# The second query-key product of two heads on 64 rows each, with the heads of a pair taking turns by unit

## Chip, cores and metric

The kernel runs on one core of one Trainium2 chip. The metric is the device time of one execution in microseconds (us). Several runs were made, and the median counts. The profile is of one execution and has its own time.

The engines are called TensorE (PE in the profile, PEld for its weight loads), VectorE (DVE), ScalarE (ACT), GpSimd (POOL) and SyncE (SP). SyncE here only issues DMA transfers.

## The reference: what is computed

It is one encoder block on a sequence of 1024 tokens of width 1024, all in float32. The core of it, shortened:

```
h = einsum('bsd,de->bse', x, w_in)              # one combined projection
q_a, k_a, v_a, z_a, q_b, k_b, v_b, z_b = split(h)
y_a = neighborhood_attention(q_a, k_a, v_a, rel_pos_bias)   # 8 heads of 64
y_b = windowed_gqa_with_sink(rotary(q_b), rotary(k_b), v_b, sink)  # 8 query, 2 key heads of 64
mixed = concatenate([y_a * silu(z_a), y_b * silu(z_b)])
x = layer_norm(alpha * x + mixed @ w_out, gain, bias)
```

Group A sees the tokens as a grid of 16 rows by 64 columns. Each query attends to a window of 8 rows by 16 columns, clamped inside the grid, with a learned bias for each relative position. Group B attends to keys at most 128 positions away, with rotary positions on q and k, and with one learned sink logit for each head that takes part in the softmax sum and brings no value.

## The kernel before

**Precision.** A float32 operand is split into a high and a low part in f16, h + l, and a product a * b is computed as three matmuls: ah * bh, ah * bl and al * bh. In the query-key product this is done in another way, which the change touches. A head has 64 dimensions, TensorE has 128 rows. For every head `split_q` (line 293) writes the high part of q into one half of a tile's 128 partitions and the low part into the other half. Head j = 0 of a pair has its high part in partitions 0 to 63, head j = 1 in 64 to 127. `split_k` (line 307) writes the high part of k into the tile `kh` and the low part into the tile `kl`, each in one half, and then copies each into the other half on GpSimd (`dup_`, line 317, the copy itself in line 319). So one matmul of the stacked q against `kh` (line 910) gives qh * kh + ql * kh, and a second one against `kl` (line 911) gives qh * kl + ql * kl. Both read all 128 rows.

**Units.** Attention is done in 128 units, listed by `unit_list` (line 837). First come 64 of group B: head pair p = 0 to 3, in it head j = 0 and 1, in it the eight blocks t of 128 queries. A unit of group B has 384 keys, and 256 for the first and the last block. Then come 64 of group A: pair p, head j, four column blocks b of 16 columns, and two halves of eight grid rows. A unit there has 11 or 12 rows of 24 or 32 columns, so 264, 288, 352 or 384 keys. In the code before, all units of a head stand together.

**Steps.** A hand-written loop (line 1271) walks over steps i, one unit a step, and fixes the order of instructions on every engine. What a step issues around the change:

- `stage_qk` (line 888): takes a PSUM bank of the kind "s", of which there are four (`bank`, line 80), runs the two query-key matmuls, and on VectorE one instruction (L920) that adds the bias or mask and takes the row minimum of the negated scores into `sn` and `nm`.
- `stage_exp` (line 926): the exponential on ScalarE (L936), which writes back into the same bank.
- `stage_tr` (line 939), one step later: ScalarE and VectorE split the probabilities into f16 parts (L946 and L947), and a DMA transposes them into the tile `tr` (L950). When L947 has ended, the bank is free for the unit four steps on.
- `stage_pv` (line 957): every fourth step, nine steps after a quad's first unit, 33 or 36 matmuls of the transposed probabilities with the values for a quad of four units (L975).
- `stage_on` (line 977) divides by the softmax sums, `stage_ot` (line 987) transposes two heads' outputs on TensorE (L995) and multiplies the gate in (L998, L1004).
- `pump_to` (line 1013): TensorE's fill, which is the matmuls of the projections still to come (L405, 512 columns each), and at the end the first of the output projection (L1122). `FILL_AT` says at which step each of them begins.

Other work waits in lists for ACT, DVE, POOL and SP, from which each step takes a few instructions (`pop`, line 173). `need` (line 183) issues at once what a step depends on: the splits of q and k of the head in lines 1307 to 1310, and the scaling of the bias tile in line 900.

**Loads.** `stage_load` (line 869) runs seven steps ahead. For group A it loads a bias tile at the first half of column blocks 0, 1 and 3 (block 2 shares the tile of block 1), and GpSimd scales it (L882). There are five bias buffers (`BR`). `gather_v` (line 830) loads the values of the next pair's column blocks, at the steps that `VA_STEP` names.

After the steps, `final` (line 1139) finishes the output projection and the layer norm.

The lines that a sentence can't say:

```
        nc.tensor.matmul(ps[:, :m], q, sl[0], start=True, stop=False)      # line 910
        nc.tensor.matmul(ps[:, :m], q, sl[1], start=False, stop=True)      # line 911
```

Of the kernel before, what the change touches and what calls it, by code (L numbers as in the profile page):

```python
# [17 lines left out]
HD = 64  # L18
# [5 lines left out]
NEG = -1e30  # L24
PSCALE = 2.0 ** 14
QSCALE = 2.0 ** -15
LTT, LPP, BP, BH, BR, ND, NA, NX, F1 = 1, 6, 2, 9, 5, 1, 1, 6, 0.2
NSPLIT, NP = 6, 2
ORDER = ["zb0", "z0", "zb1", "kb", "qb0", "z1", "qb1", "zb2", "qb2", "k0", "qb3", "zb3", "q0", "k1", "q1",
         "k2", "q2", "k3", "q3", "z2", "z3"]  # L30
# [12 lines left out]
Z3_END = 119  # L43
WIN_AT = [186, 202, 218, 234]
VA_AT = [46, 49, 52, 55]
VA_STEP = [(0, 1, 1), (0, 1, 3), (1, 0, 1), (1, 0, 3)]
WO_TAG = ("wor", "wor", "raw", "raw") + ("wr",) * 5 + ("wor", "wor", "raw", "raw", "raw", "wr", "wr")
M_AT = [105, 112, 118, 120]
WO_PRE = (9, 10, 12, 13, 14, 15)
# [18 lines left out]
def hybrid_block(ctx, tc, xT, x, wt, wv, wo, bias, sink, gain, lbias, cos, sin, bmask, out):  # L68
# [238 lines left out]
    def split_k(p, half, src, dep=None):  # L307
        sl = slice(512 * half, 512 * half + 512)
        ops = []
        prio = 0 if dep is None else 1  # L310
        eng = "pool" if dep and clock["step"] is not None else "dve"
        for j in range(2):
            a, o = slice(64 * j, 64 * j + 64), slice(64 - 64 * j, 128 - 64 * j)
            hi, lo = split_hl(lambda j=j, a=a: own("kh", p, j)[a, sl], lambda j=j, a=a: own("kl", p, j)[a, sl],
                              src[a], dep is None, eng)

            def dup_(w, j=j, a=a, o=o):
                t = own(w, p, j)
                nc.gpsimd.tensor_copy(t[o, sl], t[a, sl])  # L319

            o1 = enq("act", hi, dep, prio=prio, after=28 if dep else 0)
            o2 = enq(eng, lo, o1, prio=prio, after=32 if dep else 0)
            ops.append(o2)
            dup = [enq("pool", lambda d=dup_: d("kh"), o1, after=32 if dep else 0),
                   enq("pool", lambda d=dup_: d("kl"), o2, after=36 if dep else 0)]
            stk_ops.setdefault((p, j, half), []).extend(dup)
        return ops

# [508 lines left out]
    def unit_list():  # L837
        us = []
        for p in range(4):
            for j in range(2):  # L840
                for i in range(8):
                    us.append(("b", p, j, i, i % 2 == 1))
        for p in range(4):
            for j in range(2):
                for b in range(4):
                    for half in range(2):
                        us.append(("a", p, j, (b, half), half == 1))
        return us
# [9 lines left out]
    on = {}  # L858

    def geom(u):  # L860
        g, p, j, t, _ = u
        if g == "a":
            b, half = t
            w = WINW[b]
            return NKEY[b], [4 * w] * 3
        lo, hi = max(t - 1, 0), min(t + 2, 8)
        return 128 * (hi - lo), [128] * (hi - lo)

    def stage_load(u, i):
        g, p, j, t, _ = u  # L870
        n, _c = geom(u)
        if g == "a":
            b, half = t
            if half == 0 and b != 2:
                bulk["last"] = clock["step"] + 1
                bt = ap.tile([128, 23 * WINW[1]], F32, tag="bs", name="bias", bufs=BR)
                o, m = BOFF[b], 23 * WINW[b]
                nc.sync.dma_start(bt[:, :m], bias[2 * p + j, :, o:o + m])
                bv = bt[:, :m]
                ld = Op("sp", None, [], 1)  # L880
                ld.step = i
                op = enq("pool", lambda: nc.gpsimd.tensor_scalar(bv, bv, rsg, -1.0, op0=ALU.mult, op1=ALU.mult),  # L882
                         ld, prio=0)
                st["bias"] = bt, op
            o = 11 * WINW[b] * half
            st[u, "b"] = st["bias"][0][:, o:o + NROW[half] * WINW[b]], st["bias"][1]

    def stage_qk(u):
        g, p, j, t, _ = u
        n, _c = geom(u)  # L890
        ps = bank("s")
        m, end = n, 384
        if g == "a":
            b, half = t
            m, end = NROW[half] * WINW[b], 384 if half else 384 - WINW[1]
            q = stks["q", p, j][:, 512 * half + 128 * b:512 * half + 128 * b + 128]
            sl = [stks[w, p, j].rearrange("p (r c) -> p r c", c=GW)[
                :, 4 * half:4 * half + NROW[half], WIN0[b]:WIN0[b] + WINW[b]] for w in ("kh", "kl")]
            bias_t, op = st.pop((u, "b"))
            need(op)  # L900
            init = 3e38
        else:
            q = stks["q", f"b{p}", j][:, 128 * t:128 * t + 128]
            lo = max(t - 1, 0) * 128
            kv = p // 2
            sl = [stks[w, "b", kv][:, lo:lo + n] for w in ("kh", "kl")]
# [3 lines left out]
        nc.tensor.matmul(ps[:, :m], q, sl[0], start=True, stop=False)  # L910
        nc.tensor.matmul(ps[:, :m], q, sl[1], start=False, stop=True)  # L911
        s0 = sns[units.index(u) % 2]
        sn = s0[:, end - m:]
        if g == "b" and t < 2:
            nc.vector.tensor_copy(s0[:, 384:385], nsk[:, h:h + 1])
        elif units.index(u) == 64:
            nc.vector.memset(s0[:, 384 - WINW[1]:384], -NEG)
        nm = ap.tile([128, 1], F32, tag="nm", name="nm", bufs=6)
        c = min(p, 1) if g == "b" else 2
        nc.vector.tensor_tensor_reduce(sn[:, :m], ps[:, :m], bias_t, sg[:, c:c + 1], init,  # L920
                                       op0=ALU.add, op1=ALU.min, accum_out=nm)
        st[u, "sn"] = sn
        st[u, "ps"] = ps
        st[u, "nm"] = nm

    def stage_exp(u):
        n, _c = geom(u)
        m = n + 1 if u[0] == "b" else n
        sn, nm = st.pop((u, "sn")), st.pop((u, "nm"))
        pt = st.pop((u, "ps"))  # L930
        k = units.index(u) % 4
        if k == 0:
            st["sm"] = ap.tile([128, 4], F32, tag="sm", name="sm", bufs=4)
        sm = st["sm"]
        st[units.index(u) // 4, "sm"] = sm
        nc.scalar.activation(pt[:, :m], sn[:, :m], AF.Exp, bias=nm, scale=-1.0, accum_out=sm[:, k:k + 1])  # L936
        st[u, "p"] = pt

    def stage_tr(u):
        g, p, j, t, _ = u  # L940
        n, ch = geom(u)
        pt = st.pop((u, "p"))
        c, m = ch[0], len(ch)
# [7 lines left out]
        st[u, "tr"] = tr  # L951

    def quad(q):
        g, p, j, t, _ = units[4 * q]
        return g, p, j, t // 4 if g == "b" else t[0] // 2

    def stage_pv(q):
        ps = st[q, "o"] = bank("t")
        for m in range(4):
            u = units[4 * q + m]  # L960
            g, p, j, t, _ = u
            n, ch = geom(u)
            tr = st.pop((u, "tr"))
            c = ch[0]
# [1 line left out]
            for i in range(len(ch)):  # L966
# [4 lines left out]
                    v = [vb[:, max(t - 1, 0) + i, p // 2, e, :] for e in range(2)]  # L971
                ph, pl = tr[:c, 2 * i, :], tr[:c, 2 * i + 1, :]
                mms += [(ph, v[0]), (ph, v[1]), (pl, v[0])]
            for i, (a, b_) in enumerate(mms):
                nc.tensor.matmul(ps[:, HD * m:HD * m + HD], a, b_, start=(i == 0), stop=(i == len(mms) - 1))  # L975

    def stage_on(q):
        g, p, j, h = quad(q)
        ps = st.pop((q, "o"))
        ri = ap.tile([128, 4], F32, tag="ri", name="ri", bufs=4)  # L980
        nc.vector.reciprocal(ri, st.pop((q, "sm")))
        if j == 0:
            on[g, p, h] = ap.tile([128, 4, 2, HD], F32, tag="on", name="on", bufs=2)
        nc.vector.tensor_mul(on[g, p, h][:, :, j, :], ps[:, :4 * HD].rearrange("p (m e) -> p m e", e=HD),
                             ri.unsqueeze(2).to_broadcast([128, 4, HD]))

    def stage_ot(q):
        g, p, j, h = quad(q)
        if j == 0:
            return  # L990
        need(*stk_ops.get(f"zb{p}" if g == "b" else f"z{p}", ()))
        ps = bank("t")
        o = on.pop((g, p, h))
        for i in range(4):
            nc.tensor.transpose(ps[:, 128 * i:128 * i + 128], o[:, i].rearrange("p h e -> p (h e)"), identf)  # L995
# [275 lines left out]
    for i in range(-LD, NU + LO):  # L1271
# [31 lines left out]
        if bulk["last"] != i or (queues["sp"] and i - queues["sp"][0].born > 2):  # L1303
            pop("sp", 1 if i < 118 else 3)
        if i < NU:
            u = units[i]
            if u[3] in (0, 4):
                need(*stk_ops[f"b{u[1]}", u[2], u[3] // 4])
            if u[3] == (0, 0):
                need(*stk_ops[u[1], u[2], 0], *stk_ops[u[1], u[2], 1])  # L1310
            stage_qk(u)
        q, m = divmod(i - LP - 3, 4)
        if i >= Q30 + 2:
            q, m = (NU // 4 - 2, i - Q30 - 2) if i < Q30 + 4 else divmod(i - LP - 3, 4)
        elif i >= Q30:
            q, m = -1, 0
        if m == 0 and 0 <= q - 1 < NU // 4:
            stage_ot(q - 1)
        if m == 0 and 0 <= q < NU // 4:
            stage_pv(q)  # L1320
        if i > Z3_END:
# [9 lines left out]
            wo_scale(i - WO_MAX - 4)  # L1331
        pump_to(i + F1)
        if 0 <= q < NU // 4:
            g, p, j, h = quad(q)
            if g == "a" and p < 3 and (j, h, m) in VA_STEP:
                gather_v(p + 1, VA_STEP.index((j, h, m)))
        if m == 1 and 0 <= q < NU // 4:
            stage_on(q)
        turned = pop("dve", ND if i < M_AT[1] else 2)
# [85 lines left out]
```

## Time and profile before

| what | value |
|---|---|
| median of 3 runs | 447.07 us (446.6 to 447.26) |
| the profiled execution | 447.43 us |
| its span in the profile | 445.6 us |
| mean granted TensorE clock | 0.998 |
| units' query-key matmuls, first and last start | 123.5 and 356.7 us |

The span is what the trace covers of the profiled execution; the rest of its time lies around it. Instruction rows of the profile name the line of the kernel, the engine, the operation, output <- inputs by the program's tile names, the shape, and a count. In a group of instructions the numbers behind the bar are the busy time in us, the mean duration of one in ns, then the idle time of the engine ahead of them and what ended it. In the timeline the first number is the start in us from the span's start, the second the duration of the row, in which matmuls that follow each other directly are merged. In a table of windows each engine has its busy time, and in brackets its number of instructions; the last columns are the granted clock, the DMA share and GB/s. A matmul's end is modelled, so the distance from one start to the next says more than its duration.

### The profile page before, as it was taken

The numbers are of one execution on the slowest core, as the hardware profiler recorded it, in microseconds if no ns is written. First come the engines' busy times: TensorE is split into PE (matmuls) and PEld (weight loads), VectorE is DVE, ScalarE is ACT, GpSimd is POOL, SyncE is SP. The second block draws the span as 40 slices with busy tenths as digits, with TensorE's granted clock in tenths as the row PEclk, the third lists the DMA queues.
The fourth block names the chain that finished last, engine by engine and source line by source line (L and its number), as shares of the span: only waits on it lengthen the run. The fifth ranks groups of instructions, "written<-read, shape, count | busy, mean of one in ns | idle before, by whom it ended". The sixth has DMA issues, their size and how long they took to land.

```text
span 445.6 us, 9522 instructions
## 1 busy us (share of the span) xinstructions
PE 438.6 (98%) x3271; PEld 254.3 (57%) x3271; DVE 345.7 (78%) x862; ACT 309.0 (69%) x718; POOL 227.0 (51%) x240
## 2 busy tenths in 40 slices
PE   9999999999999999999999999999999999999994
PEld 8996754444445555565655655655555654444442
DVE  5969967829989787786898888897767747279954
ACT  6769459877488998798979978797886876002211
POOL 0002753565837758868507628667762446005740
PEclk9999999999999999999999999999999999999999
DMA  8972068976847887678989999999999888101721
GB/s 306 348 286 94 1 242 270 298 268 238 285 138 165 149 179 163 141 146 133 165 164 173 194 182 184 201 188 239 189 189 229 156 190 323 49 0 71 253 79 71
DMA packets 133984, 81.76 MB, mean 183 GB/s; under 512 B 101296, under 2 KB 113328, under 8 KB 133680
## 3 DMA queue, kind: packets, MB, share of 16 engines
q1 hardware_dynamic: 133504, 80.67, 74.1%
q8 instruction: 25, 0.41, 0.4%
q10 hardware_dynamic: 432, 0.49, 0.3%
q14 instruction: 23, 0.19, 0.2%
HBM read 50.73 MB, written 9.96 MB: 136 GB/s over the span
## 4 chain that ended last, share of the span: by engine, by line
PE 88%; DMA 6%; ACT 3%; DVE 1%; issue 0%; SPq 0%; ACTq 0%; DVEq 0%
PE ps_pj L405 47%; PE ps_s L1122 9%; PE ps_t L975 7%; PE ps_pj L1122 5%; PE ps_t L1122 5%; PE ps_s L910 4%; PE ps_s L911 4%; PE ps_s L662 3%; PE ps_t L995 2%; PE ps_t L662 1%; DMA wos<-in_wo 1%; PE ps_pj L662 1%; DMA wr<-in_wt 1%; DMA x<-in_xT 1%; ACT wf L511 1%; DMA wvraw<-in_wv 1%
## 5 line engine op out<-in xcount | busy, mean ns | idle before, releaser
L405 PE MATMUL ps_pj<-xf,wh 128*128 128x512 f16 x672 | 202.6, 379 | 0.1
L405 PE MATMUL ps_pj<-xf,wl 128*128 128x512 f16 x336 | 127.3, 379 | 0.0
L405 PEld LDWEIGHTS <-wh 128*128 128x128 f16 x672 | 63.9, 98 | 60.3 <-issue 0.5
L936 ACT ACTIVATE ps_s<-sn,nm 128x385 f32<-128x385 f32 (+3 forms) x128 | 70.0, 547 | 28.9 <-DVE nm L920 27.8
L947 DVE SCALAR_TENSOR_TENSOR split<-ps_s,split 128x384 f16<-128x384 f32 (+2 forms) x128 | 65.6, 512 | 16.9 <-ACT split L946 16.0
L1122 PEld LDWEIGHTS <-m 128*128 128x128 f16 x408 | 38.8, 98 | 42.7 <-issue 0.2
L946 ACT ACTIVATE split<-ps_s 128x384 f16<-128x384 f32 (+2 forms) x128 | 57.6, 450 | 2.4
L405 PEld LDWEIGHTS <-wl 128*128 128x128 f16 x336 | 32.9, 98 | 36.7
L920 DVE CUSTOM_DVE_ANT_0 sn<-ps_s,bias,sg 128x264 f32<-128x264 f32 (+1 forms) x64 | 35.2, 549 | 15.8 <-PE ps_s L911 5.3
L212 POOL TENSOR_SCALAR wr<-wr,wsc 128x512 f32<-128x512 f32 x26 | 22.1, 851 | 41.1 <-ACT wh L207 35.5
L920 DVE CUSTOM_DVE_ANT_0 sn<-ps_s,bm,nsk 128x384 f32<-128x384 f32 (+1 forms) x64 | 40.7, 636 | 1.8 <-PE ps_s L911 1.3
L1122 PE MATMUL ps_s<-wo,m 128*128 128x512 f16 (+1 forms) x192 | 42.0, 372 | 0.0
L910 PE MATMUL ps_s<-ks,qs 128*128 128x384 f16 (+4 forms) x128 | 39.2, 306 | 0.0
L882 POOL TENSOR_SCALAR bias<-bias,rsg 128x552 f32<-128x552 f32 (+1 forms) x24 | 18.7, 779 | 40.3 <-DMA bias<-in_bias 32.0
L911 PE MATMUL ps_s<-ks,qs 128*128 128x384 f16 (+4 forms) x128 | 39.2, 306 | 0.0
L975 PEld LDWEIGHTS <-tr 128*128 128x128 f16 (+1 forms) x1104 | 36.6, 98 | 2.2
L1179 ACT ACTIVATE sd<-mv,eps 128x1 f32<-128x1 f32 x8 | 2.4, 295 | 44.3 <-DVE mv L1177 42.0
L213 POOL TENSOR_TENSOR wl<-wr,wh 128x512 f16<-128x512 f32 x26 | 31.6, 1215 | 2.2
L1221 POOL TENSOR_TENSOR xr<-xr,gb 128x512 f32<-128x512 f32 x7 | 11.2, 1608 | 39.7 <-ACT xr L1218 39.7
L319 POOL COPY ks<-ks 64x512 f16<-64x512 f16 x40 | 26.0, 662 | 4.7 <-DVE ks L289 1.8
L558 POOL TENSOR_SCALAR xraw<-xraw,xsc 128x512 f32<-128x512 f32 x3 | 4.9, 1645 | 41.0 <-ACT xf L553 41.0
L1122 PE MATMUL ps_pj<-wo,m 128*128 128x512 f16 (+1 forms) x120 | 25.2, 347 | 0.0
(208 smaller groups left out, 840.3 us busy)
## 6 DMA issues: line engine op xcount, KB each, us to landing
ws<-in_wt SPq DMA_DIRECT2D x15, 512.0 KB, 5.7
wr<-in_wt SPq DMA_DIRECT2D x26, 256.0 KB, 3.7
bias<-in_bias SPq DMA_DIRECT2D x16, 276.0 KB, 3.4
wor<-in_wo SPq DMA_DIRECT2D x16, 256.0 KB, 3.6
xr<-in_x SPq DMA_DIRECT2D x8, 512.0 KB, 8.1
xraw<-in_xT SPq DMA_DIRECT2D x15, 256.0 KB, 5.0
out<-xr SPq DMA_DIRECT2D x14, 256.0 KB, 2.1
bias<-in_bias SPq DMA_DIRECT2D x8, 368.0 KB, 3.8
```

Of the source, the lines that this page charges most:

```text
L213: nc.gpsimd.tensor_sub(l, raw, h)
L319: nc.gpsimd.tensor_copy(t[o, sl], t[a, sl])
L405: nc.tensor.matmul(ps, a[:, k % 4, :], mv, start=(k == 0 and i == 0), stop=(k == KT - 1 and i == 2))
L662: nc.tensor.matmul(ps[:, :320], lh[1, k][:, 128 * t:128 * t + 128], rh[k][:, 320 * a:320 * a + 320], start=(k == 0 and i == 0), stop=(k == ...
L910: nc.tensor.matmul(ps[:, :m], q, sl[0], start=True, stop=False)
L911: nc.tensor.matmul(ps[:, :m], q, sl[1], start=False, stop=True)
L920: nc.vector.tensor_tensor_reduce(sn[:, :m], ps[:, :m], bias_t, sg[:, c:c + 1], init, op0=ALU.add, op1=ALU.min, accum_out=nm)
L936: nc.scalar.activation(pt[:, :m], sn[:, :m], AF.Exp, bias=nm, scale=-1.0, accum_out=sm[:, k:k + 1])
L946: nc.scalar.activation(hl[:, :m, 0, :c], src, AF.Copy, scale=PSCALE)
L947: nc.vector.scalar_tensor_tensor(hl[:, :m, 1, :c], src, PSCALE, hl[:, :m, 0, :c], op0=ALU.mult, op1=ALU.subtract)
L975: nc.tensor.matmul(ps[:, HD * m:HD * m + HD], a, b_, start=(i == 0), stop=(i == len(mms) - 1))
L1122: nc.tensor.matmul(ps, lh[:, ts], rh[:, cs], start=(e == EO[0] and i == 0), stop=(e == EO[-1] and i == 2))
```

## The change

The change has these parts.

- **Order of units.** In group B the two heads of a pair now take turns: block t of head 0, block t of head 1, and so on. In group A the four units of a column block (two heads, two halves) stand together, in the order head 0 first half, head 1 second half, head 1 first half, head 0 second half. So the units of an even and the following odd index are of different heads.
- **Query-key matmuls.** A new function `stage_mm` runs at each even step for both units: the first product of each on 128 rows into a bank of its own, then the second product of each on 64 rows only, those that hold the high part of q: rows 0 to 63 for head 0, 64 to 127 for head 1. The product ql * kl is left out thereby. `stage_qk` keeps what follows on VectorE. Two banks are taken at the even step.
- **k.** The low part of k of group A is no longer copied into the other half. The keys of group B keep the copy, since a key head serves query heads of both halves.
- **Around it.** A quad is now two blocks of two heads (group B) or one column block (group A); `slot` places its sums and outputs as the transposes need them, and `stage_ot` runs after every second quad for two of them. Bias tiles are kept for each head, with six buffers in place of five. The values of the next pair are gathered one block in each quad. The sink column is copied at the first block of a head instead of the first two. The splits of q and k are required for both heads at a pair's first step.

The diff, cut to its core:

```
-LTT, LPP, BP, BH, BR, ND, NA, NX, F1 = 1, 6, 2, 9, 5, 1, 1, 6, 0.2
+LTT, LPP, BP, BH, BR, ND, NA, NX, F1 = 1, 6, 2, 9, 6, 1, 1, 6, 0.2
...
-VA_STEP = [(0, 1, 1), (0, 1, 3), (1, 0, 1), (1, 0, 3)]
...
-            dup = [enq("pool", lambda d=dup_: d("kh"), o1, after=32 if dep else 0),
-                   enq("pool", lambda d=dup_: d("kl"), o2, after=36 if dep else 0)]
+            dup = [enq("pool", lambda d=dup_: d("kh"), o1, after=32 if dep else 0)]
+            dup.append(enq("pool", lambda d=dup_: d("kl"), o2, after=36) if dep else o2)
...
         for p in range(4):
-            for j in range(2):
-                for i in range(8):
-                    us.append(("b", p, j, i, i % 2 == 1))
+            for i in range(8):
+                for j in range(2):
+                    us.append(("b", p, j, i))
         for p in range(4):
-            for j in range(2):
-                for b in range(4):
-                    for half in range(2):
-                        us.append(("a", p, j, (b, half), half == 1))
+            for b in range(4):
+                for half, j in ((0, 0), (1, 1), (0, 1), (1, 0)):
+                    us.append(("a", p, j, (b, half)))
         return us
+
+    def slot(u):
+        return 2 * (u[3] % 2 if u[0] == "b" else u[3][1]) + u[2]
...
-            if half == 0 and b != 2:
+            key = p, j, b - (b == 2)
+            if st.get(("bias", j), (None,))[0] != key:
...
+    def stage_mm(us):
+        for u in us:
+            m, q, sl = qk_parts(u)
+            ps = st[u, "ps"] = bank("s")
+            nc.tensor.matmul(ps[:, :m], q, sl[0], start=True, stop=False)
+        for u in us:
+            m, q, sl = qk_parts(u)
+            a = slice(64 * u[2], 64 * u[2] + 64)
+            nc.tensor.matmul(st[u, "ps"][:, :m], q[a], sl[1][a], start=False, stop=True)
...
-        nc.tensor.matmul(ps[:, :m], q, sl[0], start=True, stop=False)
-        nc.tensor.matmul(ps[:, :m], q, sl[1], start=False, stop=True)
...
-        if g == "b" and t < 2:
+        if g == "b" and t == 0:
             nc.vector.tensor_copy(s0[:, 384:385], nsk[:, h:h + 1])
...
-        if j == 0:
-            on[g, p, h] = ap.tile([128, 4, 2, HD], F32, tag="on", name="on", bufs=2)
-        nc.vector.tensor_mul(on[g, p, h][:, :, j, :], ps[:, :4 * HD].rearrange("p (m e) -> p m e", e=HD),
+        if q % 2 == 0:
+            on[q // 2] = ap.tile([128, 2, 4, HD], F32, tag="on", name="on", bufs=2)
+        nc.vector.tensor_mul(on[q // 2][:, q % 2], ps[:, :4 * HD].rearrange("p (m e) -> p m e", e=HD),
...
-            u = units[i]
-            if u[3] in (0, 4):
-                need(*stk_ops[f"b{u[1]}", u[2], u[3] // 4])
-            if u[3] == (0, 0):
-                need(*stk_ops[u[1], u[2], 0], *stk_ops[u[1], u[2], 1])
-            stage_qk(u)
+            if i % 2 == 0:
+                us = units[i:i + 2]
+                for u in us:
+                    if u[3] in (0, 4):
+                        need(*stk_ops[f"b{u[1]}", u[2], u[3] // 4])
+                    if u[0] == "a" and i % 16 == 0:
+                        need(*stk_ops[u[1], u[2], 0], *stk_ops[u[1], u[2], 1])
+                stage_mm(us)
+            stage_qk(units[i])
...
-        if m == 0 and 0 <= q - 1 < NU // 4:
-            stage_ot(q - 1)
+        if m == 0 and (3 <= q < NU // 4 and q % 2 == 1 or q == NU // 4):
+            stage_ot(q - 3 if q < NU // 4 else q - 2)
...
-            g, p, j, h = quad(q)
-            if g == "a" and p < 3 and (j, h, m) in VA_STEP:
-                gather_v(p + 1, VA_STEP.index((j, h, m)))
+            g, p, b = quad(q)
+            if g == "a" and p < 3 and m == 1:
+                gather_v(p + 1, b)
```

More of the change, by code (lines that the diff above doesn't have):

```diff
@@ L860, in geom @@
     def geom(u):
-        g, p, j, t, _ = u
+        g, p, j, t = u
         if g == "a":
@@ L869, in stage_load @@
     def stage_load(u, i):
-        g, p, j, t, _ = u
+        g, p, j, t = u
         n, _c = geom(u)
@@ L883, in stage_load, with qk_parts @@
                          ld, prio=0)
-                st["bias"] = bt, op
+                st["bias", j] = key, bt, op
             o = 11 * WINW[b] * half
-            st[u, "b"] = st["bias"][0][:, o:o + NROW[half] * WINW[b]], st["bias"][1]
+            _, bt, op = st["bias", j]
+            st[u, "b"] = bt[:, o:o + NROW[half] * WINW[b]], op
+    def qk_parts(u):
+        g, p, j, t = u
+        n, _c = geom(u)
+        if g == "a":
+            b, half = t
+            q = stks["q", p, j][:, 512 * half + 128 * b:512 * half + 128 * b + 128]
+            sl = [stks[w, p, j].rearrange("p (r c) -> p r c", c=GW)[
+                :, 4 * half:4 * half + NROW[half], WIN0[b]:WIN0[b] + WINW[b]] for w in ("kh", "kl")]
+            return NROW[half] * WINW[b], q, sl
+        q = stks["q", f"b{p}", j][:, 128 * t:128 * t + 128]
+        lo = max(t - 1, 0) * 128
+        return n, q, [stks[w, "b", p // 2][:, lo:lo + n] for w in ("kh", "kl")]
+    def stage_mm(us):
[7 more added lines that the diff above has]
+            nc.tensor.matmul(st[u, "ps"][:, :m], q[a], sl[1][a], start=False, stop=True)
     def stage_qk(u):
-        g, p, j, t, _ = u
+        g, p, j, t = u
         n, _c = geom(u)
-        ps = bank("s")
+        ps = st[u, "ps"]
         m, end = n, 384
@@ L895, in stage_qk @@
             m, end = NROW[half] * WINW[b], 384 if half else 384 - WINW[1]
-            q = stks["q", p, j][:, 512 * half + 128 * b:512 * half + 128 * b + 128]
-            sl = [stks[w, p, j].rearrange("p (r c) -> p r c", c=GW)[
-                :, 4 * half:4 * half + NROW[half], WIN0[b]:WIN0[b] + WINW[b]] for w in ("kh", "kl")]
             bias_t, op = st.pop((u, "b"))
@@ L902, in stage_qk @@
         else:
[L903 to L906, printed above, removed]
             bias_t = bm[:, 128 if t == 0 else 0:(128 if t == 0 else 0) + n]
@@ L922, in stage_qk @@
         st[u, "sn"] = sn
-        st[u, "ps"] = ps
         st[u, "nm"] = nm
@@ L930, in stage_exp @@
         pt = st.pop((u, "ps"))
-        k = units.index(u) % 4
-        if k == 0:
+        k = slot(u)
+        if units.index(u) % 4 == 0:
             st["sm"] = ap.tile([128, 4], F32, tag="sm", name="sm", bufs=4)
@@ L939, in stage_tr @@
     def stage_tr(u):
-        g, p, j, t, _ = u
+        g, p, j, t = u
         n, ch = geom(u)
@@ L953, in quad @@
     def quad(q):
-        g, p, j, t, _ = units[4 * q]
-        return g, p, j, t // 4 if g == "b" else t[0] // 2
+        g, p, j, t = units[4 * q]
+        return g, p, t // 2 if g == "b" else t[0]
     def stage_pv(q):
@@ L960, in stage_pv @@
             u = units[4 * q + m]
-            g, p, j, t, _ = u
+            g, p, j, t = u
             n, ch = geom(u)
@@ L973, in stage_pv @@
                 mms += [(ph, v[0]), (ph, v[1]), (pl, v[0])]
+            o = HD * slot(u)
             for i, (a, b_) in enumerate(mms):
-                nc.tensor.matmul(ps[:, HD * m:HD * m + HD], a, b_, start=(i == 0), stop=(i == len(mms) - 1))
+                nc.tensor.matmul(ps[:, o:o + HD], a, b_, start=(i == 0), stop=(i == len(mms) - 1))
     def stage_on(q):
-        g, p, j, h = quad(q)
         ps = st.pop((q, "o"))
@@ L981, in stage_on @@
         nc.vector.reciprocal(ri, st.pop((q, "sm")))
-        if j == 0:
-            on[g, p, h] = ap.tile([128, 4, 2, HD], F32, tag="on", name="on", bufs=2)
-        nc.vector.tensor_mul(on[g, p, h][:, :, j, :], ps[:, :4 * HD].rearrange("p (m e) -> p m e", e=HD),
+        if q % 2 == 0:
+            on[q // 2] = ap.tile([128, 2, 4, HD], F32, tag="on", name="on", bufs=2)
+        nc.vector.tensor_mul(on[q // 2][:, q % 2], ps[:, :4 * HD].rearrange("p (m e) -> p m e", e=HD),
                              ri.unsqueeze(2).to_broadcast([128, 4, HD]))
     def stage_ot(q):
-        g, p, j, h = quad(q)
-        if j == 0:
-            return
+        g, p, h = quad(q)
+        h = h // 2
         need(*stk_ops.get(f"zb{p}" if g == "b" else f"z{p}", ()))
         ps = bank("t")
-        o = on.pop((g, p, h))
+        o = on.pop(q // 2).rearrange("p q m e -> p (q m e)")
         for i in range(4):
-            nc.tensor.transpose(ps[:, 128 * i:128 * i + 128], o[:, i].rearrange("p h e -> p (h e)"), identf)
+            nc.tensor.transpose(ps[:, 128 * i:128 * i + 128], o[:, 128 * i:128 * i + 128], identf)
         if g == "b":
@@ L1333, in hybrid_block @@
         if 0 <= q < NU // 4:
-            g, p, j, h = quad(q)
-            if g == "a" and p < 3 and (j, h, m) in VA_STEP:
-                gather_v(p + 1, VA_STEP.index((j, h, m)))
+            g, p, b = quad(q)
+            if g == "a" and p < 3 and m == 1:
+                gather_v(p + 1, b)
         if m == 1 and 0 <= q < NU // 4:
```

## The prediction

> **What bounds the kernel now.** I read the profile in this order: busy time, clock, chain of work that ended last.
>
> ```profile
> span 445.6 us, 9522 instructions
> ...
> PE 438.6 (98%) x3271; PEld 254.3 (57%) x3271; DVE 345.7 (78%) x862; ACT 309.0 (69%) x718; POOL 227.0 (51%) x240
> ...
> PEclk9999999999999999999999999999999999999999
> ...
> PE 88%; DMA 6%; ACT 3%; DVE 1%; issue 0%; SPq 0%; ACTq 0%; DVEq 0%
> PE ps_pj L405 47%; PE ps_s L1122 9%; PE ps_t L975 7%; PE ps_pj L1122 5%; PE ps_t L1122 5%; PE ps_s L910 4%; PE ps_s L911 4%; PE ps_s L662 3%; PE ps_t L995 2%; PE ps_t L662 1%; DMA wos<-in_wo 1%; PE ps_pj L662 1%; DMA wr<-in_wt 1%; DMA x<-in_xT 1%; ACT wf L511 1%; DMA wvraw<-in_wv 1%
> ```
>
> TensorE (PE) carries 88% of the chain, at full clock throughout. Since a busy PE need not be a PE at its peak, I went on to the timeline of PE, where the spacing of starts is the true cost of a matmul:
>
> ```profile
> 250.28 0.38 PE L405 MATMUL ps_pj<-xf,wl 128*128 128x512 f16 x1
> 250.50 0.38 PE L405 MATMUL ps_pj<-xf,wh 128*128 128x512 f16 x1
> 250.71 0.28 PE L910 MATMUL ps_s<-ks,qs 128*128 128x264 f16 x1
> 250.82 0.28 PE L911 MATMUL ps_s<-ks,qs 128*128 128x264 f16 x1
> ...
> 243.32 0.31 PE L910 MATMUL ps_s<-ks,qs 128*128 128x352 f16 x1
> 243.47 0.31 PE L911 MATMUL ps_s<-ks,qs 128*128 128x352 f16 x1
> ...
> 125.27 0.33 PE L910 MATMUL ps_s<-ks,qs 128*128 128x384 f16 x1
> 125.44 0.33 PE L911 MATMUL ps_s<-ks,qs 128*128 128x384 f16 x1
> 125.60 0.59 PE L405 MATMUL ps_pj<-xf,wh 128*128 128x512 f16 x2
> ...
> 210.37 0.27 PE L910 MATMUL ps_s<-ks,qs 128*128 128x256 f16 x1
> 210.48 0.27 PE L911 MATMUL ps_s<-ks,qs 128*128 128x256 f16 x1
> ```
>
> A record of 0.38 us is followed by the next start 0.22 us later: matmuls stream back to back, and a record outlasts its stream by about 0.16 us. A query-key matmul costs 0.165 us on the path at 384 columns (0.33 for the two from 125.27 to 125.60), 0.15 at 352, 0.11 at 264 and at 256. In the windows quoted below (130 to 160, 270 to 300 us) PE is busy in 30.00 of 30 us, and the list of waits names none of PE's between the first unit (123.5 us) and the last (356.7): here time is the sum of streams. So a saving of PE time counts fully, until a wait that is hidden now comes forward.
>
> **The change, part by part.**
>
> *The second product.* It runs once per unit on 128 rows:
>
> ```profile
> L911 PE MATMUL ps_s<-ks,qs x128: 272/320/326, 123.6 to 356.7; 128*128 128x384 f16 x64, 128*128 128x256 f16 x16, 128*128 128x264 f16 x16, 128*128 128x288 f16 x16
> ```
>
> Afterwards it reads 64 rows, the high half of q against the low part of k; the product of the two low parts goes. A 64-row matmul streams the same columns, so nothing is saved by one alone. What can be saved is the overlap: head 0's sits in rows 0 to 63, head 1's in rows 64 to 127, they write different banks and follow each other. If they run together, each pair costs the longer one and the shorter is saved: 24 pairs of 384 columns (group B), 8 of 256, and in group A 16 pairs of 264 with 288 and 16 of 352 with 384. That is 24 x 0.165 + 8 x 0.11 + 16 x 0.11 + 16 x 0.15 = 9.0 us. Check: half of L911's 4% of 445.6 us is 8.9. That they do overlap no row here shows; the bounds are 0 and 9.0. I take 9.0, since the operands and banks of the two are disjoint.
> The Trainium skill's page "TensorE: Matmul & The Clock Gate", Part 3, reports 3.07 times the rate for four 32-row matmuls packed so, which speaks for full overlap; no run here shows it yet.
>
> *Changing between 128 and 64 rows.* Each pair goes from whole-array matmuls to half-array ones and back: 64 x 2 = 128 changes. The trace of before has no 64-row matmul. The nearest rows are other changes of form:
>
> ```profile
> L405 PE MATMUL ps_pj<-xf,wh 128*128 128x512 f16 x672 | 202.6, 379 | 0.1
> ...
> 248.02 0.60 PE L995 MATMUL ps_t<-identf,on 128*128 128x128 f32 x4
> 248.45 1.12 PE L975 MATMUL ps_t<-vb,tr 128*128 128x64 f16 x33
> 249.41 0.38 PE L405 MATMUL ps_pj<-xf,wh 128*128 128x512 f16 x1
> ...
> 255.76 1.22 PE L975 MATMUL ps_t<-va,tr 96*128 96x64 f16 x36
> 256.81 0.60 PE L405 MATMUL ps_pj<-xf,wh 128*128 128x512 f16 x2
> ...
> L975 PEld LDWEIGHTS <-tr 128*128 128x128 f16 (+1 forms) x1104 | 36.6, 98 | 2.2
> ```
>
> From f32 transposes to f16 and on, 33 matmuls fit into 249.41 - 248.45 = 0.96 us, 29 ns each; the 36 at 255.76, of which half have 96 rows and half 128, take 1.05 us, again 29 ns. So these changes cost nothing. A change cannot gain, since PE already runs without holes. At the other end the array empties first: the tail of a record, 379 - 216 = 163 ns, plus an exposed weight load of 98 ns, 261 ns. I take 0, the nearer row, and keep 0 to 261 ns a change, 0 to 33 us in all. The saving is used up at 9.0 / 128 = 70 ns a change.
>
> *Both heads' first products at the even step.* The odd unit takes its bank of scores one step earlier. With four banks, unit u+3's step must find unit u's bank free, where u+4's sufficed. The bank is free when L947 of unit u ends:
>
> ```profile
> 131.81 0.33 PE L910 MATMUL ps_s<-ks,qs 128*128 128x384 f16 x1
> ...
> 136.56 0.27 PE L910 MATMUL ps_s<-ks,qs 128*128 128x256 f16 x1
> ...
> 136.65 0.55 DVE L947 SCALAR_TENSOR_TENSOR split<-ps_s,split 128x384 f16<-128x384 f32 x1
> ...
> 210.75 0.55 DVE L947 SCALAR_TENSOR_TENSOR split<-ps_s,split 128x384 f16<-128x384 f32 x1
> ...
> 281.30 0.55 DVE L947 SCALAR_TENSOR_TENSOR split<-ps_s,split 128x384 f16<-128x384 f32 x1
> ...
> 283.41 0.28 PE L910 MATMUL ps_s<-ks,qs 128*128 128x264 f16 x1
> ...
> 130.00:160.00 30.00, 30.00 (x249) 16.69 (x248) 25.35 (x84) 27.29 (x71) 21.28 (x20) 1.00 0.78 150
> 270.00:300.00 30.00, 30.00 (x282) 17.61 (x280) 25.94 (x70) 25.38 (x64) 20.66 (x27) 1.00 1.10 197
> ```
>
> Unit 5's bank is free at 137.20, and step 8 starts at 136.56: 0.64 us late, 0.5 for the second matmul of the pair. Unit 45's is free at 211.30 against step 48 at 210.37: 0.8 late. Unit 85's is free at 281.85 against 283.41: 1.6 us to spare. The same difference over all odd units (128 rows of L947, 128.7 to 359.3 us) is under 0.5 us for 13 of them, all among units 1 to 17 and 33 to 49. So PE, which waits for no bank now, will wait there, where ScalarE (27.29 of 30 us busy) and VectorE run some 5 us behind (unit 5: from its L910 at 131.8 to 137.2); after unit 50 it will not. Queued behind a waiting score matmul are the pair's others, the probability-value products and the fill of projections, all of PE. Bounds: 0, if the pair leaves ScalarE and VectorE better fed, and 6 us, if they set the pace in all of group B. I take 3.0: the 18 pairs of the two tight stretches keep nothing (18 x 0.14 = 2.5), plus 0.5 for the backlog.
>
> *Edits that cost or bring nothing on the path.*
>
> ```profile
> L319 POOL COPY ks<-ks 64x512 f16<-64x512 f16 x40 | 26.0, 662 | 4.7 <-DVE ks L289 1.8
> ...
> DVE sn L920 <- POOL ks L319: 4.2, 4, 1.4
> ...
> L995 PE MATMUL ps_t<-identf,on x64: 272/273/273, 159.2 to 370.7; 128*128 128x128 f32 x64
> ...
> bias<-in_bias SPq DMA_DIRECT2D x16, 276.0 KB, 3.4
> ...
> L882 POOL TENSOR_SCALAR bias<-bias,rsg 128x552 f32<-128x552 f32 (+1 forms) x24 | 18.7, 779 | 40.3 <-DMA bias<-in_bias 32.0
> ...
> 120.32 2.63 DVE L289 TENSOR_TENSOR qs<-rp_raw,qs 64x512 f16<-64x512 f32 x2
> ...
> 145.48 1.16 POOL L289 TENSOR_TENSOR qs<-rp_raw,qs 64x512 f16<-64x512 f32 x1
> ...
> 149.94 0.27 PE L910 MATMUL ps_s<-ks,qs 128*128 128x256 f16 x1
> ```
>
> Group A's 16 copies of kl go: 16 x 662 ns = 10.6 us off GpSimd, which is 51% busy. VectorE waits on those copies 4.2 us in all, but PE does not, so 0. The 64 transposes (L995) and 1104 probability-value matmuls keep their number; group B's quads hold 30 or 36 matmuls in place of 33. Bias loads and value gathers keep their count; both heads' bias loads now stand in adjacent steps on SP's queue, seven steps ahead, with six buffers. Seven steps of 1.84 us (123.5 to 356.7 us over 127) are 12.8 us, against 3.4 to land and 0.8 to scale, so a load that comes a step or two later is still covered; were it not, the score's reduction L920 would wait and hold its bank. The gathers go out one in each quad of the pair before, three to five quads ahead. By the code VectorE loses eight of its 16 one-column copies of the sink (L915), off the path. Both heads' q must now be split at a pair's first step; head 1's was needed eight steps later. Qb0's first half was done by 122.95 (120.32 + 2.63), 0.5 us before the first step at 123.5, and qb1's at 146.64 for step 16 at 149.94; at a pair of group A the fill leaves five steps. Without that cover the first score matmul would stall PE by what is missing.
>
> **The sum**, against the profiled execution: 445.6 - 9.0 + 0 + 3.0 = 439.6 us of span, plus the 1.8 us that lie around it (447.43 - 445.6) is 441.4. That run stands 0.36 us above the median of 447.07, which gives **441.0 us**. With waits of 0 to 6 us it is 438 to 444.
>
> **Rivals.**
> *Emptying the array (slower).* Each change waits until the array is empty and pays part or all of the 163 ns tail: at 163 ns, 447.1 - 9.0 + 128 x 0.163 = 459.0; with the weight load exposed as well 471.5. It decides from 70 ns a change; bank waits vanish, as PE comes later. Against it stand the changes above that cost nothing; for it, that none of them alters how rows are grouped: 96 rows may well use the whole array's form. At 70 ns the time is that of now.
> The Trainium skill's page "TensorEngine Tiling (Array Packing)", Key Properties, states this rule, that a change of tiling mode drains TensorE, without a price; no run here shows it so far.
> *No overlap.* The two 64-row matmuls run in turn: nothing saved, and the five odd units whose bank now comes late (1.7 us together at today's pace) give 448.8. For it: no row shows two matmuls at once. Against: disjoint rows and banks.
> *VectorE and ScalarE become the bound.* All 32 pairs of group B keep nothing (24 x 0.165 + 8 x 0.11 = 4.8) and the 1.7 us are added: 447.1 - 9.0 + 6.5 = 444.6. For it: 25.35 and 27.29 of 30 us busy. Against: lag falls after unit 17.
>
> **Chances.** My forecast, 438 to 444: 0.38. VectorE and ScalarE, 444 to 446: 0.14. Emptying: 0.40, of which 0.06 lie near 70 ns and 0.34 above, with 0.12 over 459.5. No overlap: 0.08. Hence faster 0.52, within 0.2% (0.9 us, about what a measurement of this kernel can tell) 0.06, slower 0.42. Both signs hold much, so the range runs from 438.0 to 459.5, leaving out some 0.15; the forecast's own range is 438 to 444.
>
> **What would show it.** In the timeline of after, the two 64-row matmuls should start within about 20 ns of each other, and the next whole-array matmul one stream (0.165 us at 384 columns) after them. A hole in front of the 64-row pair and another behind it, of equal size in all 64 pairs, would be the emptying; starts 0.16 us apart, no overlap. Waits of PE on L947 in the first 18 units and around unit 45 would show the banks, and their absence makes me too slow by 3 us. The kl copies should leave 24 of L319. I am wrong above all if the change between 128 and 64 rows costs 70 ns or more.

## The result, and the profile after

The changed kernel takes 453.55 us (median of 4 runs, 453.1 to 454.26) against 447.16 us for the kernel before in the same comparison: 1.0141 times as long, with a 95% interval from 1.0116 to 1.0167. It is **slower by 6.4 us**, where 441.0 us was forecast. The profiled execution took 453.1 us, its span is 451.3 us. The change shifts the line numbers: L908 and L912 are the first and second query-key product (L910 and L911 before), L404 the fill (L405), L963 the split on VectorE that sets a bank free (L947).

The page of the changed kernel, the rows that answer to those shown of before:

```profile
span 451.3 us, 9483 instructions
...
PE 442.9 (98%) x3271; PEld 242.0 (54%) x3271; DVE 344.9 (76%) x854; ACT 309.3 (69%) x718; POOL 219.0 (49%) x224
...
PE 68%; issue 9%; ACT 8%; POOL 7%; DVE 6%; DMA 1%; SPq 0%; POOLq 0%; DVEq 0%; ACTq 0%
...
L908 PE MATMUL ps_s<-ks,qs 128*128 128x384 f16 (+4 forms) x128 | 29.6, 306 | 1.5 <-DVE split L963 1.3
```

TensorE is "busy" 98% as before, with as many matmuls, and its busy time grew by 4.3 us although half of the second products now lie beside others. In the chain of work 9% is "issue", time in which an engine waited for nothing that the profile shows, against 0% before. That share is not the loss: of its 38.5 us, 26.1 lie before the first query-key product (122.5 us, against 123.5 before), where there is no 64-row matmul yet and the kernel is not late. The chain has only gone another way there. The list of waits of TensorE's weight loads says where to look (columns: who waited for whom, us in total, times, longest):

```profile
PEld L912 <- issue: 20.1, 64, 1.2
PEld L404 <- issue: 6.7, 39, 0.2
```

There are 64 waits ahead of L912, which is one in every pair. Their 20.1 us hold the streams that ran meanwhile and are no price either. The timeline of PE shows a pair, and below it that of the weight loads in the same place:

```profile
129.01 0.49 PE L908 MATMUL ps_s<-ks,qs 128*128 128x384 f16 x2
129.43 0.34 PE L912 MATMUL ps_s<-ks,qs 64*128 64x384 f16 x2
129.70 0.61 PE L404 MATMUL ps_pj<-xf,wh 128*128 128x512 f16 x2
```

```profile
128.80 0.31 PEld L908 LDWEIGHTS <-qs 128*128 128x128 f16 x2
129.43 0.10 PEld L912 LDWEIGHTS <-qs 64*128 64x128 f16 x2 [0.32 <-issue]
129.70 0.11 PEld L404 LDWEIGHTS <-wh 128*128 128x128 f16 x2 [0.17 <-issue]
```

Read the starts. From 129.01 two matmuls of 384 columns stream, 2 x 0.163 us, until 129.33; the 64-row pair starts at 129.43, 0.10 us later. Both of its matmuls are in a row of 0.34 us, the length of one: they overlap. They stream 0.163 us, until 129.59, and the next whole-array matmul starts at 129.70, again 0.10 us later. The weight loads tell the same. L908's first load begins at 128.80, 0.21 us ahead of its matmul; those of L912 and of the L404 behind it begin only when their matmul does. At a change between the whole array and half of it (a change of form, from here on) no weights are loaded ahead. A row of PE hides this, since a matmul's record outlasts its stream by 0.16 us and covers a hole of 0.10.

Adding up all matmuls from the first query-key product to the last gives the whole price. In the traces a matmul of n columns streams n x 0.417 ns + 2.5 ns (384 columns 162.5 ns, 512 columns 215.8; PE's starts in the kernel before agree to 0.5 us in 233). What a start comes later than that is a hole, summed here by what stands on both sides; stretch is the time from the first to the end of the last:

| kernel | median us | ahead of first products (banks) | ahead of 64 rows | behind 64 rows | saved by overlap | stretch us |
|---|---|---|---|---|---|---|
| before | 447.16 | 0.0 | | | | 233.3 |
| changed | 453.55 | 2.4 | 6.1 (64, 96 ns each) | 6.6 (64, 104 ns each) | 8.75 | 239.3 |

12.7 us of holes and 2.4 us of bank waits against 8.75 us saved make 6.4 us. Two small things are not in this sum: the second matmul behind a 64-row pair starts some 10 ns late too (0.7 us in all), and the kernel before has 0.4 us of holes. With them the starts give 6.6 us, so they answer for the measured time to 0.3 us. (The stretch grew by 6.0 only, since three matmuls of the fill, 0.65 us, now fall outside it.)

The bank waits are five, at units 7, 9, 13, 17 and 49. For the longest these rows of PE's timeline of the changed kernel stand. The pair's second unit starts 1.05 us after the first, 0.89 more than a stream, and its row names the split of the unit four before:

```profile
142.91 0.33 PE L908 MATMUL ps_s<-ks,qs 128*128 128x384 f16 x1
143.96 0.32 PE L908 MATMUL ps_s<-ks,qs 128*128 128x384 f16 x1 [0.73 <-DVE split L963]
```

### The profile page after: what moved, and what is told of

It is laid out like the page before. It is cut to its first block, busy times and chain, and to the rows that moved or that the text cites. A ratio compares the mean times of both kernels' runs of the same rounds, so it can differ in the third digit from the quotient of the medians.

```text
span 451.3 us, 9483 instructions
## 1 busy us (share of the span) xinstructions
PE 442.9 (98%) x3271; PEld 242.0 (54%) x3271; DVE 344.9 (76%) x854; ACT 309.3 (69%) x718; POOL 219.0 (49%) x224
## 4 chain that ended last, share of the span: by engine, by line
PE 68%; issue 9%; ACT 8%; POOL 7%; DVE 6%; DMA 1%; SPq 0%; POOLq 0%; DVEq 0%; ACTq 0%
PE ps_pj L404 26%; PE ps_s L1137 9%; PE ps_t L992 6%; PE ps_pj L1137 5%; PE ps_t L1137 5%; PE ps_s L908 3%; PE ps_s L661 3%; POOL wl L212 3%; PE ps_s L912 3%; PE ps_s L607 2%; POOL wr L211 2%; ACT ps_s L952 2%; DVE sn L937 2%; PE ps_t L661 1%; PE ps_pj L661 1%
## 5 line engine op out<-in xcount | busy, mean ns | idle before, releaser
L404 PE MATMUL ps_pj<-xf,wh 128*128 128x512 f16 x672 | 202.3, 380 | 0.0
L404 PE MATMUL ps_pj<-xf,wl 128*128 128x512 f16 x336 | 127.4, 379 | 0.0
L404 PEld LDWEIGHTS <-wh 128*128 128x128 f16 x672 | 60.2, 98 | 67.9 <-issue 6.1
L963 DVE SCALAR_TENSOR_TENSOR split<-ps_s,split 128x384 f16<-128x384 f32 (+2 forms) x128 | 65.5, 512 | 20.3 <-ACT split L962 19.9
L962 ACT ACTIVATE split<-ps_s 128x384 f16<-128x384 f32 (+2 forms) x128 | 57.6, 450 | 2.4
L404 PEld LDWEIGHTS <-wl 128*128 128x128 f16 x336 | 32.9, 98 | 37.9 <-issue 0.7
L937 DVE CUSTOM_DVE_ANT_0 sn<-ps_s,bias,sg 128x264 f32<-128x264 f32 (+1 forms) x64 | 35.1, 549 | 17.4 <-PE ps_s L912 16.4
L908 PE MATMUL ps_s<-ks,qs 128*128 128x384 f16 (+4 forms) x128 | 29.6, 306 | 1.5 <-DVE split L963 1.3
L952 ACT ACTIVATION_READ_ACCUMULATOR ps_s<-sn,nm 128x1 f32 x128 | 24.4, 191 | 0.2
L661 PEld LDWEIGHTS <-xf 128*128 128x128 f16 x192 | 18.3, 98 | 8.2 <-ACT xf L534 0.6
```

The costliest lines, as they stand in the source:

```text
L404: nc.tensor.matmul(ps, a[:, k % 4, :], mv, start=(k == 0 and i == 0), stop=(k == KT - 1 and i == 2))
L661: nc.tensor.matmul(ps[:, :320], lh[1, k][:, 128 * t:128 * t + 128], rh[k][:, 320 * a:320 * a + 320], start=(k == 0 and i == 0), stop=(k == ...
L962: nc.scalar.activation(hl[:, :m, 0, :c], src, AF.Copy, scale=PSCALE)
L963: nc.vector.scalar_tensor_tensor(hl[:, :m, 1, :c], src, PSCALE, hl[:, :m, 0, :c], op0=ALU.mult, op1=ALU.subtract)
```

## The experiments

The theory to be tested: **each change between whole-array and half-array matmuls costs 0.10 us**, since the array empties and the next weights are loaded only then. The runs test the price and what it hangs on, not what the 0.10 us is made of. The rivals: the turns of the heads cost the time (order of units, banks, loads), the 64-row form is slow as such, or the holes belong to two tiles side by side. The runs stand in an order that takes the change apart, then multiplies its parts. The kernel before took 446.94 us in the comparisons of the first, second, third and fifth run below, and 447.31 us in those of the fourth, sixth and seventh; differences are taken from the one that belongs to the run.

**The turns without the 64 rows.** In the changed kernel:

```
-            dup = [enq("pool", lambda d=dup_: d("kh"), o1, after=32 if dep else 0)]
-            dup.append(enq("pool", lambda d=dup_: d("kl"), o2, after=36) if dep else o2)
+            dup = [enq("pool", lambda d=dup_: d("kh"), o1, after=32 if dep else 0),
+                   enq("pool", lambda d=dup_: d("kl"), o2, after=36 if dep else 0)]
...
-            a = slice(64 * u[2], 64 * u[2] + 64)
-            nc.tensor.matmul(st[u, "ps"][:, :m], q[a], sl[1][a], start=False, stop=True)
+            nc.tensor.matmul(st[u, "ps"][:, :m], q, sl[1], start=False, stop=True)
```

> The changed kernel with the second product on all 128 rows again and kl copied into both halves again; the heads still take turns and both units' matmuls still come at the even step. Theory (emptying: each change between 128 and 64 rows costs 0.10 us, 0.20 a pair, while the overlap saves its 9 us): without any change nothing is paid and nothing saved, so the time is that of before plus the waits for banks taken a step early, 1.5 to 2.4 us: 448.6 to 449.6, and the holes around the second products are gone. Rival (the turns themselves cost it: the order of units, early banks, bias and value loads side by side): 453, as the changed kernel.

Measured: 450.11 us, 1.0073 [1.0059, 1.0086] of before. The holes around the second products are gone; in PE's timeline of this kernel (L911 is the second product here, L962 the split) two of 352 or 384 columns follow two others after 0.31 us and the fill after another 0.31, streams without a gap:

```profile
261.57 0.47 PE L908 MATMUL ps_s<-ks,qs 128*128 128x352 f16 x2
261.88 0.47 PE L911 MATMUL ps_s<-ks,qs 128*128 128x352 f16 x2
262.19 0.59 PE L404 MATMUL ps_pj<-xf,wh 128*128 128x512 f16 x2
```

What is left, 3.2 us, is above the expected 1.5 to 2.4: the list of waits has 2.4 us of L908 for the split, and the sum of starts finds 3.4 us ahead of first products, in six waits, since a record covers the first 0.16 us of each. So the turns cost 3.2 us, and the 64 rows add the other 3.2 of the 6.4 us (by the starts, 4.0 more in holes than the overlap saves, and 1.0 less in bank waits).

```profile
PE ps_s L908 <- DVE split L962: 2.4, 4, 1.1
```

**The turns, each unit at its own step.** One line of that kernel differs, so that no bank is taken early:

```
-                stage_mm(us)
+            stage_mm(units[i:i + 1])
```

> As the first kernel of this call, but each unit's two matmuls (128 rows) at the unit's own step, so no bank is taken early. Theory (emptying): the bank waits go too and only the order of units is left: 447.2, give or take 0.9. If the order of units costs by itself: above 448.1. Rival (turns cost it all): about 453.

Measured: 447.61 us, 1.0018 [1.0007, 1.003]. Of the 3.2 us, 2.5 were the early banks. What is left is 0.7 us (0.3 to 1.3 by the interval) for the order of units with its loads, and the starts hold 0.8 us ahead of first products, in three waits for a bank.

**64 rows without the turns.** In the kernel before, the second product alone:

```
-        nc.tensor.matmul(ps[:, :m], q, sl[1], start=False, stop=True)
+        a = slice(64 * j, 64 * j + 64)
+        nc.tensor.matmul(ps[:, :m], q[a], sl[1][a], start=False, stop=True)
```

> The kernel before, in which only the second product reads 64 rows, the high half of q; heads do not take turns, so no two 64-row matmuls of different halves follow each other. The copies of kl stay. Theory (emptying): 128 units change twice, 256 x 0.10 = 25.6 us, nothing is saved: 472.7 and a hole of 0.10 us on each side of every second product. Rival (the hole belongs to two tiles working side by side, not to the change of rows): 447.2.

Measured: 474.17 us, 1.0615 [1.0601, 1.063]: 27.2 us for 256 changes, 106 ns each, where 25.6 was expected. Nothing stands beside these matmuls, so the hole does not belong to two tiles at once. PE's timeline of this kernel, one unit, with 0.10 us on each side of L912 (streams 0.163):

```profile
261.91 0.33 PE L910 MATMUL ps_s<-ks,qs 128*128 128x384 f16 x1
262.17 0.33 PE L912 MATMUL ps_s<-ks,qs 64*128 64x384 f16 x1
262.43 0.66 PE L996 MATMUL ps_t<-identf,on 128*128 128x128 f32 x4
```

The hole is the same whatever stands behind: 100 to 104 ns ahead of f32 transposes as ahead of the fill. The second matmul behind it comes late once more, by 10 ns in the fill and by 51 to 59 ns among the f32 transposes (four take 0.66 us here, 0.60 in the kernel before). That is 2.1 us in all, and with it the starts give 27.5 us for the 27.2 measured.

**96 rows.** The 128-row turns (the first kernel above), with `q[0:96], sl[1][0:96]` in the second product.

> The first kernel of the call before (heads take turns, both units at the even step) with the second product on rows 0 to 95 for both heads, so for head 1 it takes rows that partly hold the low part of q and its sum is another one. Theory (only a change between whole-array and half-array form empties the array; 96 rows use the whole array's form): no holes, no overlap, 450.1 give or take 0.5. Rival (any matmul on fewer than 128 rows makes a change): 128 holes of 0.10 us, 462.9.

Measured: 450.29 us, 1.0072 [1.0053, 1.0092], the time of its 128-row partner. In PE's timeline of this kernel the 96-row pair streams without a gap (264 and 288 columns, 0.23 us from start to start, and 0.24):

```profile
263.74 0.40 PE L908 MATMUL ps_s<-ks,qs 128*128 128x264 f16 x2
263.97 0.40 PE L911 MATMUL ps_s<-ks,qs 96*128 96x264 f16 x2
264.21 0.59 PE L404 MATMUL ps_pj<-xf,wh 128*128 128x512 f16 x2
```

So fewer than 128 rows cost nothing as such. Here 96 rows go with the whole array's form, and 64 do not.

**The 64-row pass twice.** In the changed kernel:

```
-        for u in us:
+        for n, u in enumerate(us + us):
...
-            nc.tensor.matmul(st[u, "ps"][:, :m], q[a], sl[1][a], start=False, stop=True)
+            nc.tensor.matmul(st[u, "ps"][:, :m], q[a], sl[1][a], start=False, stop=n > 1)
```

> The changed kernel with the pair's two 64-row matmuls issued twice in a row (head 0, head 1, head 0, head 1), so the low part of k counts twice in the scores. Theory (emptying at a change between 128 and 64 rows only, full overlap of the halves): one more overlapped stream a pair, 9.0 us, and no more holes: 462.5. If the halves do not overlap at all: 18 us more, 471.5. If every switch between the upper and lower half empties the array too: two more holes a pair on top, 475.

Measured: 461.19 us, 1.0324 [1.031, 1.0338]. That is 14.2 us above before, 7.9 more than the changed kernel is. Four half-array matmuls take two streams and still two holes, as PE's timeline of this kernel shows: 2 x 0.163 + 0.10 = 0.43 us from L912 to the fill.

```profile
262.02 0.50 PE L912 MATMUL ps_s<-ks,qs 64*128 64x352 f16 x4
262.45 0.61 PE L404 MATMUL ps_pj<-xf,wh 128*128 128x512 f16 x2
```

Switching between the upper and the lower half costs next to nothing, then: the second pass starts some 10 ns late. The time is 1.1 us short of the expected 9.0; the bank waits shrink by more than that as TensorE comes later, to 0.5 us from 2.4.

**Its partner, the 128-row second product twice**, made of the first kernel in the same way.

> The first kernel of the call before with the second product of both units issued twice on 128 rows, so the low part of k counts twice in the scores. It is the partner of the run with the 64-row pass twice (461.2). Theory (a change costs 0.10 us whatever stands between two of them, and each pass of two halves saves a stream of 0.14): 128 more streams of 0.143 us are 18.3, less bank waits of up to 2.4 that a later TensorE no longer meets: 466.0 to 468.4, so with two passes a change the 64-row form is the faster one by 5 to 7 us. Rival (the 64-row form is slower as such): below 461.

Measured: 464.75 us, 1.0394 [1.0372, 1.0417], 17.4 us above before and below the expected range. The bank waits of its partner, 3.4 us and not the 2.4 that I had put in, are gone altogether (0.0 us in the sum of starts), so the sum is 450.1 - 3.4 + 18.3 = 465.0. The point of the run holds, with a smaller gain than the expected 5 to 7 us: with two passes to a change the half-array form is **faster by 3.2 us** (14.2 above its before against 17.4), where with one pass it is slower by 3.2 (6.4 against 3.2). The sum of starts says why: four streams of 0.143 us are 0.57 us a pair, two streams of the longer unit and two holes 0.50. That is 4.3 us in 64 pairs, less the 0.5 us of bank waits that only the half-array kernel still has. The second product twice on 128 rows in PE's timeline:

```profile
263.94 0.47 PE L908 MATMUL ps_s<-ks,qs 128*128 128x352 f16 x2
264.26 0.79 PE L911 MATMUL ps_s<-ks,qs 128*128 128x352 f16 x4
264.88 0.59 PE L404 MATMUL ps_pj<-xf,wh 128*128 128x512 f16 x2
```

**64 rows in group B only.** The first kernel with `a = slice(64 * u[2], 64 * u[2] + 64) if u[0] == "b" else slice(0, 128)`.

> The first kernel of the call before with 64 rows in the second product of group B's 32 pairs only; group A keeps 128 rows, and kl is copied into both halves. Theory (cost and saving add up by pairs): 32 x 0.20 = 6.4 us of holes, 24 x 0.165 + 8 x 0.11 = 4.8 us saved, 1.6 on top of 450.1: 451.7. Then group A's share of the changed kernel's time is the other 1.9. Rival (bank waits of group B hide the holes): 450.1.

Measured: 451.37 us, 1.0094 [1.0075, 1.0113]. That is 4.1 us above before, where the sum gives 3.2 + 1.6 = 4.8; but its interval overlaps that of the 128-row kernel, so the time alone doesn't settle it. The list of waits of the weight loads does: 32 waits ahead of L912, one for each of the 32 pairs of group B (the sum of starts below has 3.1 us ahead of them, 95 ns each; behind them it also holds one single wait of about 1 us).

```profile
PEld L912 <- issue: 11.7, 32, 1.2
```

All kernels in one table, by the sum of starts (us):

| kernel | median | banks | ahead of 64 | behind 64 | stretch |
|---|---|---|---|---|---|
| turns, own step, 128 rows | 447.61 | 0.8 | | | 233.9 |
| turns, 128 rows | 450.11 | 3.4 | | | 235.8 |
| turns, 96 rows | 450.29 | 3.4 | | | 236.0 |
| turns, 64 rows in group B | 451.37 | 2.5 | 3.1 | 4.4 | 238.0 |
| 64-row pass twice | 461.19 | 0.5 | 6.1 | 5.9 | 246.7 |
| 128-row second product twice | 464.75 | 0.0 | | | 250.6 |
| 64 rows, no turns | 474.17 | 0.0 | 12.3 | 13.2 | 260.4 |

No kernel beat the one before. By estimate from these figures, two pairs to a change would save 0.13 us in every four units (2 x 0.163 - 0.20), at most 4 us in all, but need the banks of four units at once; there are four banks, and taking one of them a step early already cost 2.5 us. It wasn't tried.

## Why the prediction was wrong

**The bound.** Right: TensorE streams almost without holes before (0.4 us in 233), so its time counts fully. That a busy share says little of it held for the changed kernel as well.

**The overlap.** Right, and to size: 9.0 us forecast, 8.75 measured; the two halves start 3 ns apart. The Trainium skill's page "TensorE: Matmul & The Clock Gate", Part 3, gives about 4 ns for tiles of different rows; the trace agrees.

**The changes between 128 and 64 rows. This is the step that failed.** The prediction took 0 ns a change, "the nearer row", from transposes to f16 matmuls and from 96 to 128 rows, and kept 261 ns as the other end. Measured are 96 ns going in and 104 ns coming out, 12.7 us in 128 changes, above the 70 ns at which it said the saving is used up. The rows that it took for near were near in the wrong respect: the run with 96 rows shows that going between 96 and 128 rows is no change of form. The prediction had seen the doubt ("96 rows may well use the whole array's form") and put it into a rival with a chance of 0.40 rather than into the sum. What did happen is what that rival, the emptying, foretold, a hole on each side of all 64 pairs, at 100 ns instead of its 163: 447.1 - 9.0 + 128 x 0.10 + 2.4 = 453.3 us. The record's tail of 163 ns was the wrong price for it: the hole is shorter, and the same for 256 and for 384 columns. What the 0.10 us is made of stays open: by the records the new load begins 91 ns after the computed end of the stream ahead and the matmul 4 ns later, while the record of the matmul ahead, whose end is modelled, still runs for 67 ns. So the traces show the hole and the late load, but not the emptying itself. The Trainium skill's page "TensorEngine Tiling (Array Packing)", Key Properties, has the rule that a change of tiling mode drains TensorE; the trace agrees in so far as each of the 128 changes has its hole, 96 ns going in and 104 ns coming out on average.

**The banks.** Forecast 3.0 us, where the saving of TensorE would meet a late VectorE. Measured 2.4 in the changed kernel and 3.4 by the starts (2.5 in time) with 128 rows. The size is near and the place is right, since the banks waited for are those of units 3, 5, 9, 13 and 45, all in the two tight stretches. The working was not: it let all 18 pairs there lose their saving of 0.14 us, while five waited, for 0.25 to 0.89 us. That the sums lie close is in part luck. (Its lateness of unit 45 is 0.93 us where that of unit 5 is 0.64, 211.30 against 210.37; the 0.8 counts from the pair's second matmul.) The rival's half-sentence that the waits vanish when TensorE comes later was wrong for holes of 0.2 us a pair; they all but vanish only in the kernels that are 14 us and more behind.

**The edits at no cost.** Right as far as the runs show: holes, bank waits and overlap answer for the time to 0.3 us, which leaves no more than that for the 16 copies less on GpSimd (24 of L318 are left) and the eight less on VectorE; no run takes them by themselves. The order of units, with the bias and value loads, costs about 0.7 us.

**No overlap, and VectorE and ScalarE as the bound:** neither came. 453.55 lies inside the range of 438.0 to 459.5, which reached to the emptying; the forecast itself, 441.0, had the wrong sign.

## What to carry to other kernels

Half-array matmuls in the upper and lower rows do run side by side (their starts are 3 ns apart), but going into that form and out of it costs about 0.10 us each way, so where TensorE is the bound, a pass must save more than about 0.20 us before it pays: at 384 columns one overlapped pair saves 0.16, two save 0.33. In this kernel's mix of columns one pass lost 3.2 us against the same pass on 128 rows, and two won 3.2. Collect the half-array matmuls behind each other, or leave them on the whole array. And when a term of the sum has no row of its own, ask in what respect the nearest row is near: the change from f32 to f16 and from 96 to 128 rows cost nothing here, and said nothing of 64 rows.

## What the runs showed of the hardware that was not expected

A matmul on 96 rows counts as one on the whole array (450.29 us against 450.11 with 128 rows), one on 64 does not. At a change of form the load of the weights starts only once the stream ahead has been over for some 91 ns, 4 ns ahead of its matmul, where the first load of L908 starts 0.21 us ahead of its own. The hole does not show as idle time of PE: its records are modelled ends and cover it, so it is found in the distance between starts and in the weight loads' wait for "issue".
